# Moving the normalisation, the accumulation and layer-two buffers in a two-layer attention encoder

## The chip, the core and the metric

The kernel runs on one core of one Trainium2 chip. The metric is the device time in microseconds of one launch, from host input to output in the chip's memory, as a median over runs. The engines are TensorE (PE; its weight loads are shown apart as PEld), VectorE (DVE), ScalarE (ACT), GpSimd (POOL) and SyncE (SP), which issues the DMAs.

## What is computed

The reference is an encoder of two layers over 1024 tokens of width 1024, in fp32, with 256 memory tokens. Each layer normalises its input, projects it once, runs groups of attention heads, multiplies their joined output by SiLU of a gate, projects it and adds it to the input; a last RMSNorm follows.

```python
h = rmsnorm(x, norm_g)
... = _split(h @ w_in, SPLITS)
y = concatenate([heads of the layer, y_x], -1) * silu(gate)
return x + y @ w_out
```

In layer one the groups are A (six heads, window of 128 to each side, a bias by relative position, a learned sink in the softmax), B (six dense heads with normalised and rotated queries and keys) and X (four heads of cross-attention into the memory). In layer two they are C and X. C is differential attention, six heads with values of width 128:

```python
p = softmax(s + bias)
w = p[0] - lam * p[1]
y_c = rmsnorm(w @ v, subln_g) * (1.0 - lam_init)
```

## The kernel before

**Arithmetic.** TensorE is fed with fp32 numbers split into a high and a low part (the names end in h and l); a product is three matmuls (high·high, high·low, low·high), some with two where one side's low part is left out. A projection is 48 matmuls of 128x512: two halves of 512 tokens, each 24 matmuls into one accumulator `acc` (L292). Its weights come by DMA (`wr`), DVE makes the high part `wh` (L236), POOL or DVE the low part `wl` (L238).

**Projections as filling.** The projections of a layer are a list of jobs, with steps before which a job may not start (`after`). `jobs.pull(n)` runs the next n pieces of eight matmuls, `jobs.ensure(tag)` runs the list until a job is done. So attention steps and projections are mixed by hand in one program order; a scheduler then settles the order on each engine from readiness and priority, so the built order is not quite the source's.

**Attention steps.** `run_steps` (L432) takes a list of steps, each one block of 128 queries of a head (256 for A). In pass i it does, in this order:

- the hop of step i-1 (`word_copy`, L497): a DMA on SP that copies the finished map `e` to `er`, in the number format in which TensorE transposes it;
- s1 of step i: the scores on PE into an S bank (`sx`, `sb`, `sa`, `sc`), the row minimum on DVE, the exponential on ACT with the row sums, and the normalisation of the map: on DVE for X, on POOL for B and A (L1019, L1098). For C, DVE adds the bias while it takes the minimum (L1384), and after two exponentials (L1387) comes rz (L1391), a factor mr (L1393) and the combination of the two maps, e = e2 * mr + e1 (L1395);
- s3 of an older step: the product with the values on PE into an A bank (`ox`, `ob`, `oa`, `oc`) and its evacuation. Behind C's s3 lie two posts, each called in a pass of its own: sums of squares `ssqc` in a T bank (L1424), z from them on DVE (L1427), a power on POOL (L226); then the broadcast `rbcc` in a T bank (L1436) and O = O * rbcc on DVE (L1438);
- the first half of the step's filling (`fill` is 3 pieces for X, C and B's first head, 1 for the rest);
- the posts;
- s2 of an older step (lag 2, for most A and B steps 3): eight transposes of `er` in two groups into T banks (`te`, L514; `ta` for A), each copied out by ACT (PTh, L306) and DVE (PTl, L307);
- the second half of the filling.

**Buffers.** PSUM has three pairs: S (two of 128x1024), T and A (two of 128x512 each). T also takes the transposed values `tv` (L396) and the posts' tiles; A also takes the projections' `acc`. In SBUF, `er` has three buffers in both layers, and the rings of a layer are set in `open_main` (L349 to 354), for layer two Q with 6 (the queries `cq`), `sg` with 3 (a projection's split result), K 4, KL 2, V 2, gy 2 (the gates).

**Layer two's list of jobs** (from L1306) is xq0, xq1 (the queries of X), m0 to m3 (keys and values of the memory), the gates g6 and g7 for X, then per head k, q, v and gate, each not before a given step (q0 not before step 8, v0 not before step 9). `jobs.ensure("m1")` (L1344) runs the list up to m1 before the first of the eight X steps; the 48 C steps follow.

Of the kernel before, what the change touches and what calls it, by code (L numbers as in the profile page):

```python
# [38 lines left out]
SLOW = (4,)  # L39
XB = 0  # L40
ABLAG = 3
ER = 3
PRE = (range(2, 8), range(2, 4))
SPARE = 24

# [107 lines left out]
def encoder_kernel(ctx, tc, A):  # L153
    nc = tc.nc
# [33 lines left out]
    gq, nlam, gs, ls, le = (misc[:, a:b] for a, b in ((0, 1), (1, 2), (2, 3), (3, 5), (5, 7)))  # L188
# [32 lines left out]
    def stat(name, n=1, bufs=3):  # L221
        return sm.tile([P, n], F32, tag=name, name=name, bufs=bufs)
# [209 lines left out]
    def run_steps(steps, jobs, hooks=None):  # L432
        n = len(steps)
        posts = deque()
        p2 = p3 = 0
        for i in range(n + LAG + 1):
            if jobs is not None:
                jobs.step = i
            if hooks:
                hooks(i)  # L440
            if 0 < i <= n and steps[i - 1].hop:
                steps[i - 1].hop()
            if i < n:
# [12 lines left out]
            if jobs is not None:  # L456
                jobs.pull(f - f // 2)
            for q in list(posts):
                q.pop(0)()
                if not q:  # L460
                    posts.remove(q)
            if p2 < n and p2 + steps[p2].lag <= i:
                steps[p2].s2()
                p2 += 1
            if jobs is not None:
# [30 lines left out]

    def word_copy(M, e):  # L497
        def f():
            t = M.at.tile([P, 1024], F32R, tag="er", name="er", bufs=ER)
            dma(t.bitcast(F32), e[0])  # L500
            e[0] = t
        return f
# [39 lines left out]
    def x_steps(M, X, gates, fill, qtile, ydst):  # L542
        steps = []
        for qb in range(8):
# [5 lines left out]
            e = [None]  # L550
            st.fill = fill

            def s1(qb=qb, e=e):
                kh, kl = X["kh"], X["kl"]
                Sp = ps_s("sx").rearrange("p (h m) -> p h m", h=4)
                for h in range(4):
                    qt, qc = qtile(h, qb)
                    qk(Sp[:, XPOS[h], :], qt, qc, kh[:, h, :], kl[:, h, :], 0, MEM)
                mn = stat("mn4", 4)
                nc.vector.tensor_reduce(out=mn, in_=Sp, op=ALU.min, axis=AX.X)  # L560
                et = new_e(M)
                ev = et.rearrange("p (h m) -> p h m", h=4)
                z = stat("z4", 4)
                for h in range(4):
                    nc.scalar.activation(ev[:, h, :], Sp[:, h, :], AF.Exp, bias=mn[:, h:h + 1],
                                         scale=-1.0, accum_out=z[:, h:h + 1])
                rz = stat("rz4", 4)
                nc.vector.reciprocal(rz, z)
                for h in range(4):
                    nc.vector.tensor_scalar(out=ev[:, h, :], in0=ev[:, h, :], scalar1=rz[:, h:h + 1],  # L570
                                            scalar2=None, op0=ALU.mult)
                e[0] = et
            st.s1 = s1
            st.hop = word_copy(M, e)
            st.s2 = dense_s2(M, e, st)
# [94 lines left out]
    M = open_main(right, "right", 0)  # L670
# [133 lines left out]
    def load_q(store, src, h):  # L804
        store[h] = new_q(M, "q")
        dma(store[h], src[h])
# [68 lines left out]
    def gt(l, m, after=-1):  # L875
        add(l, jl, "g%d" % m, gate_job(m), after)
# [27 lines left out]
    jobs = Jobs(jl, ld)  # L904
# [73 lines left out]
    last_x = steps[7].s1  # L978

    def x7():  # L980
        last_x()
        jobs.ensure("bq0")
        load_q(Bq, bq_d, 0)
    steps[7].s1 = x7
    bgrp = {}
    if True:
        def b_step(h, qb):
# [8 lines left out]
            def s1(h=h, qb=qb, e=e):  # L996
                if qb == 2 and h < 5:
                    jobs.ensure("bq%d" % ((h + 1) // 2))
                    load_q(Bq, bq_d, h + 1)
                if h == NB0 and qb == 0:  # L1000
                    jobs.ensure("bq2")
                    open_ab()
                    jobs.ensure("aq0")
                    load_q(Aq, aq_d, 0)
                    a_bias(0)
                Sp = ps_s("sb")
                for j in range(2):
# [8 lines left out]
                nc.scalar.activation(et, Sp, AF.Exp, bias=mr, scale=nrq[:, qb, h:h + 1], accum_out=z)  # L1016
                rz = stat("rz")
                nc.vector.reciprocal(rz, z)  # L1018
                nc.gpsimd.tensor_tensor(out=et, in0=et, in1=rz.to_broadcast([P, 1024]), op=ALU.mult)  # L1019
                e[0] = et  # L1020
            st.s1 = s1
            st.hop = word_copy(M, e)
            st.s2 = dense_s2(M, e, st)
# [35 lines left out]
    if True:  # L1059
        def a_step(h, p):  # L1060
# [5 lines left out]
            def s1(h=h, p=p, e=e):  # L1066
# [23 lines left out]
                nc.vector.tensor_tensor(out=z, in0=z, in1=es, op=ALU.add)  # L1090
                rz = stat("rz2", 2)
                nc.vector.reciprocal(rz, z)
                for j in range(2):
                    qb = 2 * p + j
                    lo, hi = max(0, qb - 1) * P, min(8, qb + 2) * P
                    c = lo - (qb - 1) * P
                    ej = et[:, j, c:c + hi - lo]
                    nc.gpsimd.tensor_tensor(out=ej, in0=ej, in1=rz[:, j:j + 1].to_broadcast([P, hi - lo]), op=ALU.mult)  # L1098
                e[0] = et
            st.s1 = s1  # L1100

            def hop(p=p, e=e):
                t = M.at.tile([P, 1024], F32R, tag="er", name="er", bufs=ER)[:, :768]
# [203 lines left out]
        add(1, jl, "xq%d" % p, lambda w, p=p: proj_job(w, hT, S, half_q(Xq1, p, lambda m: m)))  # L1307
    for tag, src, run in mem_jobs(M, 1, memT, X):
        job(jl, tag, src, run)
    gt(1, 6)  # L1310
    gt(1, 7)
    for h in range(6):
        a = -1 if h == 0 else 8 + 8 * (h - 1)
        add(1, jl, "k%d" % h, ck_job(h), a)
        add(1, jl, "q%d" % h, lambda w, h=h: proj_job(w, hT, S, half_q(C[h], 0, lambda m: m)),
            8 if h == 0 else a + 4)
        if h < 5:
            add(1, jl, "v%d" % h, v_job(C[h], True), 9 if h == 0 else 8 + 8 * (h - 1) + 1)
            gt(1, h, 9 if h == 0 else a + 2)
# [29 lines left out]
    for h in range(6):  # L1349
        for qb in range(8):  # L1350
# [8 lines left out]
            def s1(h=h, qb=qb, e=e, grp=grp):  # L1359
# [20 lines left out]
                for m in range(2):  # L1380
# [6 lines left out]
                    nc.scalar.activation(et, et, AF.Exp, bias=mn[:, m:m + 1], scale=-1.0,  # L1387
                                         accum_out=z[:, m:m + 1])
                    es.append(et)
                rz = stat("rz")  # L1390
                nc.vector.reciprocal(rz, z[:, 1:2])  # L1391
                c = stat("mr")
                nc.vector.scalar_tensor_tensor(out=c, in0=z[:, 0:1], scalar=nlam, in1=rz,  # L1393
                                               op0=ALU.mult, op1=ALU.mult)
                nc.vector.scalar_tensor_tensor(out=es[0], in0=es[1], scalar=c, in1=es[0],  # L1395
                                               op0=ALU.mult, op1=ALU.add)
# [132 lines left out]
```

## Time and profile before

| | |
|---|---|
| median of three runs | 1284.13 us (1282.78 to 1285.4) |
| profiled execution | 1293.23 us |
| its span (first to last instruction) | 1291.4 us |
| its mean granted TensorE clock | 0.983 |
| moved by DMA | 198.85 MB, 154 GB/s on average |

Times of a view are microseconds from the start of the span. A row of instructions shows start, duration, engine, line, operation and tiles, and in brackets the wait ahead of it with the instruction that ended it. A row of waits shows who waited for whom, then the total, the number and the longest. By the starts of their matmuls on PE, layer one's scores and products lie between 66.7 us (the first `sx`) and 551.8 (the last `oa`), the first parts of its output projection (`pre`, L631) from 441.1, layer two's products `ox` end at 725.3, and its C steps lie between 707.4 (the first `sc`) and 1217.4 (the last `oc`).

### The profile page before, as it was taken

The page shows a single profiled execution, that of the slowest core. Times are in us where ns is not written, and L with a number is a line of the kernel's source. Part 1 is how long each engine was busy: PE and PEld are TensorE (multiplying, and loading weights), DVE is VectorE, ACT ScalarE, POOL GpSimd, SP SyncE. Part 2 cuts the span into 40 slices and gives each one's busy share as a digit, 9 for nine tenths or more (in the row PEclk, how much of TensorE's full clock was granted, in tenths as well). Part 3 has the DMA queues.
Part 4 walks back from the last instruction along what each step waited for, and adds up shares of the span by engine and source line. Part 5 has one row for each costly group of instructions (what it writes and reads, how often), then busy time and mean ns, then how long its engine had stood idle before and what let it go on. Part 6 is the DMA issues. An engine that isn't in the chain of part 4 may idle for free.

```text
span 1291.4 us, 19572 instructions
## 1 busy us (share of the span) xinstructions
PE 1231.4 (95%) x6806; PEld 1006.6 (78%) x6806; DVE 854.2 (66%) x1623; ACT 605.0 (47%) x1275; POOL 425.3 (33%) x390
## 2 busy tenths in 40 slices
PE   5989999999999899999999999999999999999998
PEld 4878888888887678877787787777777777876886
DVE  5566676477777787747466856776767676676444
ACT  6245464356566755633134534444444444464222
POOL 5024355356666654503032122231222122131100
PEclk9999999999999899999999999999999999997999
DMA  6654335545365555377544333342332323453263
GB/s 245 196 177 152 130 140 183 166 149 194 135 226 204 202 204 192 143 220 258 145 163 129 130 101 104 114 119 100 115 120 99 119 100 106 139 196 124 83 212 120
DMA packets 95646, 198.85 MB, mean 154 GB/s; under 512 B 11286, under 2 KB 30998, under 8 KB 95548
## 3 DMA queue, kind: packets, MB, share of 16 engines
q1 hardware_dynamic: 95548, 197.60, 45.9%
q8 instruction: 54, 0.88, 0.3%
q14 instruction: 44, 0.36, 0.1%
HBM read 78.80 MB, written 30.95 MB: 85 GB/s over the span
## 4 chain that ended last, share of the span: by engine, by line
PE 45%; DVE 4%; issue 2%; DMA 1%; ACT 1%; POOL 0%; POOLq 0%; SPq 0%; DVEq 0%; ACTq 0%
PE acc L292 22%; PE po L631 5%; PE oc L1409 5%; PE sc L1372 3%; PE te L514 3%; PE sc L1378 2%; PE pre L631 2%; DVE wh L236 1%; PE ssqc L1424 1%; PE ox L588 1%; DVE e L1395 1%; DVE O L1438 1%; ACT e L1387 1%; DMA wor<-in_w_out 0%; PE tv L396 0%
## 5 line engine op out<-in xcount | busy, mean ns | idle before, releaser
L292 PE MATMUL acc<-h,wh 128*128 128x512 f32 x1536 | 497.2, 399 | 5.9 <-DVE wh L236 2.0
L292 PEld LDWEIGHTS acc<-h,wh 128*128 128x128 f32 x1536 | 284.6, 190 | 64.7 <-issue 7.2
L292 PE MATMUL acc<-h,wl 128*128 128x512 f32 x768 | 307.1, 400 | 1.6 <-POOL wl L238 1.6
L238 POOL TENSOR_TENSOR wl<-wr,wh 128x512 fp32r<-128x512 f32 x96 | 125.9, 1313 | 283.6 <-DVE wh L236 144.5
L292 PEld LDWEIGHTS acc<-h,wl 128*128 128x128 f32 x768 | 145.7, 190 | 35.0 <-issue 5.8
L1387 ACT ACTIVATE e<-e,mn 128x1024 f32<-128x1024 f32 x96 | 110.2, 1149 | 130.4 <-DVE mn L1384 130.4
L307 DVE TENSOR_TENSOR PTl<-te,PTh 128x512 fp32r<-128x512 f32 x224 | 145.6, 684 | 32.4 <-ACT PTh L306 31.0
L306 ACT CAST PTh<-te 128x512 fp32r<-128x512 f32 x224 | 124.4, 588 | 76.4 <-PE te L514 71.9
L1384 DVE CUSTOM_DVE_ANT_0 e<-sc,toep 128x1024 f32<-128x1024 f32 x96 | 113.9, 1219 | 24.7 <-PE sc L1378 24.6
L1019 POOL TENSOR_TENSOR e<-e,rz 128x1024 f32<-128x1024 f32 x48 | 92.2, 1922 | 72.6 <-DVE rz L1018 68.8
L514 PEld LDWEIGHTS te<-identr,er 128*128 128x128 f32 x896 | 93.5, 144 | 26.9 <-DVE O L1438 12.2
L514 PE MATMUL te<-identr,er 128*128 128x128 f32 x896 | 102.8, 251 | 7.4 <-DVE O L1438 3.2
L236 DVE CAST wh<-wr 128x512 fp32r<-128x512 f32 x112 | 61.8, 554 | 38.6 <-PE acc L292 18.6
L226 POOL TENSOR_TENSOR rz<-z,nhalf 128x2 f32<-128x2 f32 x24 | 16.7, 697 | 198.5 <-DVE z L1427 192.6
L1016 ACT ACTIVATE e<-sb,mr,nrq 128x1024 f32<-128x1024 f32 x48 | 58.0, 1208 | 43.1 <-DVE mr L1015 34.1
L1409 PE MATMUL oc<-PTh,v 128*128 128x256 f32 x384 | 74.8, 288 | 0.0
L631 PE MATMUL po<-woh,yh 128*128 128x512 f32 (+1 forms) x176 | 67.9, 387 | 0.1
L631 PE MATMUL po<-woh,yl 128*128 128x512 f32 (+1 forms) x176 | 67.3, 383 | 0.0
L631 PE MATMUL po<-wol,yh 128*128 128x512 f32 (+1 forms) x176 | 67.3, 382 | 0.0
L1409 PEld LDWEIGHTS oc<-PTh,v 128*128 128x128 f32 x384 | 61.4, 191 | 6.2 <-issue 5.5
L1395 DVE SCALAR_TENSOR_TENSOR e<-e,mr 128x1024 f32<-128x1024 f32 x48 | 65.3, 1360 | 0.9
L1011 DVE TENSOR_REDUCE mn<-sb 128x1 f32<-128x1024 f32 x48 | 58.4, 1216 | 6.3 <-PE sb L483 6.1
(199 smaller groups left out, 2289.7 us busy)
## 6 DMA issues: line engine op xcount, KB each, us to landing
er<-e SPq DMA_DIRECT2D x112, 512.0 KB, 3.0
wr<-in_w_in SPq DMA_DIRECT2D x96, 256.0 KB, 2.8
ysc<-gy SPq DMA_DIRECT2D x16, 512.0 KB, 2.8
wor<-in_w_out SPq DMA_DIRECT2D x32, 256.0 KB, 3.7
cq<-sg SPq DMA_DIRECT2D x64, 128.0 KB, 2.4
ck<-sg SPq DMA_DIRECT2D x48, 128.0 KB, 2.4
er<-e SPq DMA_DIRECT2D x12, 384.0 KB, 2.6
xt<-in_x SPq DMA_DIRECT2D x8, 512.0 KB, 6.2
```

The source lines that it names most:

```text
L236: nc.vector.tensor_copy(hi, raw)
L238: (nc.vector if fast else nc.gpsimd).tensor_tensor(out=lo, in0=raw, in1=hi, op=ALU.subtract)
L292: lastmm[0] = nc.tensor.matmul(acc, a, b[:, k, c0:c0 + n], start=(i == 0), stop=(i == 23))
L306: nc.scalar.copy(hi, src)
L307: return nc.vector.tensor_tensor(out=lo, in0=src, in1=hi, op=ALU.subtract)
L514: nc.tensor.transpose(to[:, i * P:(i + 1) * P], e[0][:, k * P:(k + 1) * P], idt)
L631: lastmm[0] = nc.tensor.matmul(acc, a, b, start=(start and n == 0), stop=(stop and n == 2))
L1019: nc.gpsimd.tensor_tensor(out=et, in0=et, in1=rz.to_broadcast([P, 1024]), op=ALU.mult)
L1384: nc.vector.tensor_tensor_reduce(out=et, in0=Sp, in1=toeps[h][:, w0:w0 + 1024], scale=1.0, scalar=BIG, op0=ALU.add, op1=ALU.min, accum_out ...
L1387: nc.scalar.activation(et, et, AF.Exp, bias=mn[:, m:m + 1], scale=-1.0, accum_out=z[:, m:m + 1])
L1395: nc.vector.scalar_tensor_tensor(out=es[0], in0=es[1], scalar=c, in1=es[0], op0=ALU.mult, op1=ALU.add)
L1409: nc.tensor.matmul(acc, V[:, kt, v, :], pt[:, kt, :], start=(n == 0), stop=(n == 23))
```

## The change

Three things are edited.

First, in `run_steps` the normalisation is taken out of s1: each s1 returns it as `finish`, which is called after s2. Second, s3 goes behind the first half of the filling and the posts. Third, in layer two `er` gets two buffers instead of three, Q eight instead of six and `sg` five instead of three; gate 6 is listed right behind m1 (ahead of m2 and m3) and must be done before the steps start, and q0 may start at step 4 instead of 8.

```diff
@@ open_main
-        M.cfg = (dict(Q=(1024, 4), K=4, KL=4, V=1, gy=4, sg=3) if l == 0
-                 else dict(Q=(512, 6), K=4, KL=2, V=2, gy=2, sg=3))
+        M.cfg = (dict(Q=(1024, 4), K=4, KL=4, V=1, gy=4, sg=3, er=3) if l == 0
+                 else dict(Q=(512, 8), K=4, KL=2, V=2, gy=2, sg=5, er=2))
@@ run_steps
-                steps[i].s1()
+                finish = steps[i].s1()
+            f = steps[min(i, n - 1)].fill
+            if jobs is not None:
+                jobs.pull(f - f // 2)
+            for q in list(posts):
+                q.pop(0)()
+                if not q:
+                    posts.remove(q)
             if p3 < n and p3 + steps[p3].lag + 1 <= i:
                 st, p3 = steps[p3], p3 + 1
                 if st.s3 is not None:
...
                     r = st.s3()
                     if r:
                         posts.append(r)
-            f = steps[min(i, n - 1)].fill
-            if jobs is not None:
-                jobs.pull(f - f // 2)
-            for q in list(posts):
-                q.pop(0)()
-                if not q:
-                    posts.remove(q)
             if p2 < n and p2 + steps[p2].lag <= i:
                 steps[p2].s2()
                 p2 += 1
+            if finish:
+                finish()
+                finish = None
             if jobs is not None:
                 jobs.pull(f // 2)
@@ the s1 of C (those of X, B and A likewise)
-                rz = stat("rz")
-                nc.vector.reciprocal(rz, z[:, 1:2])
...
-                e[0] = es[0]
+                def finish():
+                    rz = stat("rz")
+                    nc.vector.reciprocal(rz, z[:, 1:2])
...
+                    e[0] = es[0]
+                return finish
@@ the jobs of layer two
     for tag, src, run in mem_jobs(M, 1, memT, X):
         job(jl, tag, src, run)
-    gt(1, 6)
+        if tag == "m1":
+            gt(1, 6)
     gt(1, 7)
...
-            8 if h == 0 else a + 4)
+            4 if h == 0 else a + 4)
...
-    jobs.ensure("m1")
+    jobs.ensure("m1", "g6")
```

In the changed kernel a line has another number, up to some 15 away, than before. The built orders show what moves. First, DVE in layer two, in a C step without s3; before (rz, mr and e as above; sg is the low part of a projection's result, O the scaled product of the pair before, PTl the low part of a transposed map):

```order
L1391 RECIPROCAL rz_10254<-mn_10121 128x1
L1438 SCALAR_TENSOR_TENSOR O_10169<-O_10169,misc_84,rbcc_10285 128x256
L1393 SCALAR_TENSOR_TENSOR mr_10256<-mn_10121,misc_84,rz_10254 128x1
L310 SCALAR_TENSOR_TENSOR sg_10276<-acc_10226,sg_10275 128x512
L1395 SCALAR_TENSOR_TENSOR e_10248<-e_10251,mr_10256,e_10248 128x1024
L307 TENSOR_TENSOR PTl_10210<-te_10290,PTh_10208 128x4x128
```

Now, from rz on in the same step:

```order
L1403 RECIPROCAL rz_10276<-mn_10095 128x1
L1440 SCALAR_TENSOR_TENSOR z2_10258<-ssqc_10255,es_10176 128x2
L1405 SCALAR_TENSOR_TENSOR mr_10278<-mn_10095,misc_84,rz_10276 128x1
L1407 SCALAR_TENSOR_TENSOR e_10232<-e_10235,mr_10278,e_10232 128x1024
L306 TENSOR_TENSOR PTl_10180<-te_10262,PTh_10178 128x4x128
```

The combination e stays ahead of PTl. The copy sg and the scaling O, which stood between rz and e, have left, and z2 of the earlier pair has come in.

Second, PE in layer one, at the first A step; before (te transposes of a B step, sa and sb scores of A and B):

```order
L514 MATMUL te_2640<-identr_74,er_2357 128x128 x4
L514 MATMUL te_2647<-identr_74,er_2357 128x128 x4
L483 MATMUL sa_2656<-ak0_2207,q_2546 128x256
L483 MATMUL sa_2656<-akl0_2209,q_2546 128x256
L483 MATMUL sb_2727<-bk0_1031,q_1865 128x512
L483 MATMUL sa_2656<-ak0_2207,q_2546 128x384
L483 MATMUL sa_2656<-akl0_2209,q_2546 128x384
```

Now:

```order
L517 MATMUL te_2644<-identr_74,er_2357 128x128 x4
L486 MATMUL sa_2656<-ak0_2235,q_2546 128x256
L486 MATMUL sa_2656<-akl0_2237,q_2546 128x256
L291 MATMUL acc_2670<-h_122,wh_2448 128x512
L291 MATMUL acc_2670<-h_123,wh_2448 128x512
L291 MATMUL acc_2670<-h_122,wl_2449 128x512
L291 MATMUL acc_2670<-h_122,wh_2448 128x512
L291 MATMUL acc_2670<-h_123,wh_2448 128x512
L486 MATMUL sa_2656<-ak0_2235,q_2546 128x384
```

Between the two score groups of the A step stand five matmuls of a projection where the score of the next B step stood, and the second group of transposes has moved away.

Third, PE in the same C step as in the first pair; before:

```order
L1436 MATMUL rbcc_10285<-ident_69,rz2_10206 128x128 x2
L514 MATMUL te_10290<-identr_74,er_10119 128x128 x4
L292 MATMUL acc_10317<-h_6363,wh_10100 128x512
L292 MATMUL acc_10317<-h_6364,wh_10100 128x512
L514 MATMUL te_10297<-identr_74,er_10119 128x128 x4
```

Now:

```order
L291 MATMUL acc_10238<-h_6365,wh_9917 128x512
L1437 MATMUL ssqc_10255<-ones2_76,sqc_10174 128x2 x2
L517 MATMUL te_10262<-identr_74,er_10093 128x128 x4
L517 MATMUL te_10269<-identr_74,er_10093 128x128 x4
L291 MATMUL acc_10238<-h_6366,wh_9917 128x512
```

The two groups of transposes stand together with the sums of squares ahead of them, where the broadcast rbcc stood ahead and projections lay between them.

More of the change, by code (lines that the diff above doesn't have):

```diff
@@ L41 @@
 ABLAG = 3
-ER = 3
 PRE = (range(2, 8), range(2, 4))
@@ L464, in run_steps @@
                 p2 += 1
+            if finish:
+                finish()
+                finish = None
             if jobs is not None:
@@ L498, in f @@
         def f():
-            t = M.at.tile([P, 1024], F32R, tag="er", name="er", bufs=ER)
+            t = M.at.tile([P, 1024], F32R, tag="er", name="er", bufs=M.cfg["er"])
             dma(t.bitcast(F32), e[0])
@@ L566, in s1 @@
                                          scale=-1.0, accum_out=z[:, h:h + 1])
[L567 to L572, printed above, removed]
+                def finish():
+                    rz = stat("rz4", 4)
+                    nc.vector.reciprocal(rz, z)
+                    for h in range(4):
+                        nc.vector.tensor_scalar(out=ev[:, h, :], in0=ev[:, h, :], scalar1=rz[:, h:h + 1],
+                                                scalar2=None, op0=ALU.mult)
+                    e[0] = et
+                return finish
             st.s1 = s1
@@ L980, in x7 @@
     def x7():
-        last_x()
+        r = last_x()
         jobs.ensure("bq0")
         load_q(Bq, bq_d, 0)
+        return r
     steps[7].s1 = x7
@@ L1016, in s1, with finish @@
                 nc.scalar.activation(et, Sp, AF.Exp, bias=mr, scale=nrq[:, qb, h:h + 1], accum_out=z)
-                rz = stat("rz")
-                nc.vector.reciprocal(rz, z)
-                nc.gpsimd.tensor_tensor(out=et, in0=et, in1=rz.to_broadcast([P, 1024]), op=ALU.mult)
-                e[0] = et
+                def finish():
+                    rz = stat("rz")
+                    nc.vector.reciprocal(rz, z)
+                    nc.gpsimd.tensor_tensor(out=et, in0=et, in1=rz.to_broadcast([P, 1024]), op=ALU.mult)
+                    e[0] = et
+                return finish
             st.s1 = s1
@@ L1089, in s1, with finish @@
                 nc.scalar.activation(es, mn, AF.Exp, bias=sinkb[:, h:h + 1], scale=1.0)
[L1090 to L1099, printed above, removed]
+                def finish():
+                    nc.vector.tensor_tensor(out=z, in0=z, in1=es, op=ALU.add)
+                    rz = stat("rz2", 2)
+                    nc.vector.reciprocal(rz, z)
+                    for j in range(2):
+                        qb = 2 * p + j
+                        lo, hi = max(0, qb - 1) * P, min(8, qb + 2) * P
+                        c = lo - (qb - 1) * P
+                        ej = et[:, j, c:c + hi - lo]
+                        nc.gpsimd.tensor_tensor(out=ej, in0=ej, in1=rz[:, j:j + 1].to_broadcast([P, hi - lo]), op=ALU.mult)
+                    e[0] = et
+                return finish
             st.s1 = s1
             def hop(p=p, e=e):
-                t = M.at.tile([P, 1024], F32R, tag="er", name="er", bufs=ER)[:, :768]
+                t = M.at.tile([P, 1024], F32R, tag="er", name="er", bufs=M.cfg["er"])[:, :768]
                 a, b = (P if p == 0 else 0), (768 - P if p == 3 else 768)
@@ L1389, in s1, with finish @@
                     es.append(et)
[L1390 to L1396, printed above, removed]
-                e[0] = es[0]
+                def finish():
+                    rz = stat("rz")
+                    nc.vector.reciprocal(rz, z[:, 1:2])
+                    c = stat("mr")
+                    nc.vector.scalar_tensor_tensor(out=c, in0=z[:, 0:1], scalar=nlam, in1=rz,
+                                                   op0=ALU.mult, op1=ALU.mult)
+                    nc.vector.scalar_tensor_tensor(out=es[0], in0=es[1], scalar=c, in1=es[0],
+                                                   op0=ALU.mult, op1=ALU.add)
+                    e[0] = es[0]
+                return finish
             st.s1 = s1
```

## Prediction

> **What bounds the kernel now.** I read the page first, for the engines' shares.
>
> ```profile
> span 1291.4 us, 19572 instructions
> PE 1231.4 (95%) x6806; PEld 1006.6 (78%) x6806; DVE 854.2 (66%) x1623; ACT 605.0 (47%) x1275; POOL 425.3 (33%) x390
> ```
>
> TensorE is the bound; 60 us of the span (1291.4 - 1231.4) are left to it as idle time. An edit that moves no matmul out can only win from those 60 us, from gaps hidden under the modelled ends of matmuls, and from stretches at a lower clock. So the second view was a table by stage (stretch, its length, PE busy, granted clock, DMA share, GB/s):
>
> ```profile
> 205.00:420.00 215.00, 209.26 (x1227) 1.00 0.53 180
> 420.00:444.00 24.00, 19.66 (x109) 0.82 0.55 193
> 444.00:562.00 118.00, 115.35 (x684) 0.99 0.53 185
> 632.00:650.00 18.00, 14.71 (x92) 0.91 0.44 127
> 650.00:718.00 68.00, 65.43 (x358) 1.00 0.47 149
> 842.40:924.80 82.40, 80.44 (x449) 1.00 0.34 111
> 1155.00:1165.70 10.70, 6.86 (x47) 1.00 0.72 243
> 646.90:650.30 3.40, 3.40 (x13) 0.51 0.61 163
> 1165.70:1182.70 17.00, 17.00 (x47) 0.50 0.33 113
> ```
>
> The first three rows are layer one's mixed A and B steps, with 5.74, 4.34 and 2.65 us of PE idle. Rows four and five are the start of layer two, with 3.29 and 2.57 us. The sixth is one head of layer two: 1.96 us idle in 82.4. Row seven is the end of layer two's attention, 3.84 us idle. The last two rows lie in stretches where the granted clock was half. Third, who PE waited for in three of these stretches (205 to 420, 632 to 718, 718 to 1150; total us, times, longest):
>
> ```profile
> PE sb L483 <- ACT e L1016: 1.7, 2, 0.9
> PE acc L292 <- DVE gy L417: 1.3, 2, 0.8
> PE sa L483 <- ACT e L1016: 1.0, 1, 1.0
> PE oa L1135 <- ACT PTa L306: 0.6, 2, 0.3
> ```
>
> ```profile
> PE acc L292 <- DVE yt L596: 1.5, 2, 1.1
> PE sx L483 <- ACT e L565: 1.4, 1, 1.4
> PE ox L588 <- DVE ckl L1280: 1.0, 1, 1.0
> ```
>
> ```profile
> PE tv L396 <- DVE PTl L307: 4.2, 4, 1.1
> PE te L514 <- DVE O L1438: 3.2, 8, 0.6
> ```
>
> Nothing large is left: these are waits of about a microsecond each, nearly all for a PSUM bank that ACT or DVE has not emptied.
>
> **The change, part by part.** No arithmetic is removed or added. Three things move.
>
> *The normalisation (finish).* The words of the change put it behind the step's copies out of PSUM. In layer two the built order on DVE, shown above, does not do that: the combination (e) still stands ahead of the copy PTl; what left the stretch is the copy of the projection (sg), and the statistic of the earlier pair (z2 in place of O) came in. I cost the moved combination at nothing in both layers. The hop that follows it takes this long:
>
> ```profile
> er<-e SPq DMA_DIRECT2D x112, 512.0 KB, 3.0
> ```
>
> In layer two the copy is read two steps later, some 20 us (an 82.4 us head has eight steps), so 3.0 us and a wait for one of now two er buffers stay covered; were that cover gone, each step would pay up to 3.0 us. What queues behind a waiting hop on SP are weight loads and row copies for projections a step or more away.
>
> *The accumulation (s3) behind the first half of the fill.* In the order shown for TensorE at the first A step, projections now stand where the next score sb stood, and the trace shows what sb cost there:
>
> ```profile
> 253.79 1.20 ACT L1016 ACTIVATE e<-sb,mr,nrq 128x1024 f32<-128x1024 f32 x1
> 253.92 0.28 PE L483 MATMUL sa<-akl,q 128*128 128x256 f32 x1
> 255.13 0.50 PE L483 MATMUL sb<-bk,q 128*128 128x512 f32 x1 [0.93 <-ACT e L1016]
> ```
>
> A score needs one of two S banks, which the exponential was still reading. The two groups of waits on ACT e (1.7 + 1.0 us) should go, and part of the waits for gy and for PTa, since projections now lie between ta and oa: of 5.74 + 2.65 us I take 4.0 (ends 0 and 8.4). The stretch 420 to 444 has no projections left to fill with in either order, so its 4.34 us stay.
>
> In layer two the pieces around te move, as the third pair of orders shows. The second te needs the T bank that rbcc held till O, and now one that ssqc holds till z2. One such step of before:
>
> ```profile
> 904.79 0.73 PE L292 MATMUL acc<-h,wh 128*128 128x512 f32 x2
> 908.36 0.18 ACT L1387 ACTIVATION_READ_ACCUMULATOR e<-e,mn 128x1 f32 x1
> 908.58 0.16 DVE L1391 RECIPROCAL rz<-mn 128x1 f32<-128x1 f32 x1 [0.47 <-ACT e L1387]
> 908.69 0.55 PE L514 MATMUL te<-identr,er 128*128 128x128 f32 x4
> 909.46 0.47 DVE L1438 SCALAR_TENSOR_TENSOR O<-O,misc,rbcc 128x256 f32<-128x256 f32 x1
> 909.99 0.53 PE L514 MATMUL te<-identr,er 128*128 128x128 f32 x4 [0.22 <-DVE O L1438]
> ```
>
> O ended at 909.93. z2 would follow rz directly and, at an estimated 0.16 like rz (both a few elements wide), end near 908.9; PE comes to its second te after 908.69 plus the first four transposes, about 909, so the wait goes. Of 3.2 us I take 2.0, since some of the eight were set by weight copies that stand ahead of rz. The larger wait, 4.2 us of tv, stays: it ends with PTl, and PTl still waits for the combination.
>
> ```profile
> 891.01 1.72 DVE L1395 SCALAR_TENSOR_TENSOR e<-e,mr 128x1024 f32<-128x1024 f32 x1
> 892.65 1.28 DVE L307 TENSOR_TENSOR PTl<-te,PTh 128x512 fp32r<-128x512 f32 x2
> 893.38 0.33 PE L396 MATMUL tv<-ident,vraw 128*128 128x128 f32 x1 [1.05 <-DVE PTl L307]
> ```
>
> Ends for this term: a gain of 7.4 (both rows) and the loss of the third rival. At the end of layer two (1155 to 1165.7) DVE's order is the same as before, two weight subtractions ahead of the maps' first pass, so I take 0 of the 3.84 us.
>
> *The start of layer two.* Gate 6 (48 matmuls, as any projection) now precedes the cross-attention steps, so they start with their keys landed and with fill ready; eight Q and five sg buffers let both xq projections finish, where six and three made the last halves wait for steps that had not begun. Projections are only exchanged in time: q0, released at step 4 and not 8, fills the hole that gate 6 leaves. I take all 3.29 us of 632 to 650, the 1.0 us of ox, and 1.7 us for the half-clock stretch that follows them (half of 3.4): 6.0 (ends 3.3 and 7.6). Against it, two pairs of cross-attention steps now have both ox groups around a te with no projection between; each can make the next projection wait for its A bank as in the row acc <- yt, about 1.0 each: -2.0 (ends 0 and -4).
>
> Sum: 4.0 + 2.0 + 6.0 - 2.0 = 10.0 us. The profiled execution took 1293.23 us, 1.8 more than its span and 9.1 above the median of 1284.13; no row says what the 9.1 are, so I take the 10.0 off the median: **1274.1**, written as 1274.
>
> **The clock.** Half clock from 1165.7 to 1182.7 cost 8.5 us, right behind idle times of 3.84 us in 10.7, of which the longest single wait was about 2 us:
>
> ```profile
> PE sc L1372 <- DVE mn L1384: 2.0, 1, 2.0
> ```
>
> [...]
>
> **Rivals.**
>
> 1. *The clock gives more* (0.17). If the waits ahead of 1165.7 shrink a little, the 17 us stretch at half clock goes too: 8.5 + 3.84 more, 1261.8. For: the dips stand behind the densest waits. Against: DVE's order there is unchanged.
>
> 2. *The waits are only rearranged* (0.17). S, T and A keep two banks each, so waits taken off one place come back at the next. Then the terms 4.0 and 2.0 are nothing and -2.0 doubles: 6.0 - 4.0 = 2.0, 1282.1, no change. [...] This is also the case in which the change does not do what its words say.
>
> 3. *Slower* (0.13): z2 now stands behind rz, and rz behind the second exponential, in each of the 24 pairs of layer two, with no projections between the two te. If ACT has one more copy ahead (0.59, like PTh) and DVE one weight copy (0.43), the second te waits about 1.02 - 0.2 = 0.8 us each time: 24 x 0.8 = 19 us against gains of 4.0 + 6.0 - 2.0 = 8, so 1295. It decides from 0.33 us a step (8/24).
>
> ```profile
> 909.27 0.59 ACT L306 CAST PTh<-te 128x512 fp32r<-128x512 f32 x1 [0.73 <-PE te L514]
> 907.68 0.43 DVE L236 CAST wh<-wr 128x512 fp32r<-128x512 f32 x1
> ```
>
> **The numbers.** The forecast itself (1266 to 1281) has 0.53. Faster by over 0.2% (2.6 us, about what a measurement of this kernel can tell from no change) holds it and rival 1: 0.70; within: 0.17; slower: 0.13. The range 1260 to 1286 takes in rivals 1 and 2 and leaves out rival 3 and some of the deeper ends of rival 1, under 2 in 10.
>
> **What would show it.** Right: no wait of sb on ACT e between A and B steps; 632 to 650 with under 1 us idle and full clock; te <- O gone; tv <- PTl still near 1 us a head. Wrong: tv <- PTl gone, a row te <- z of many microseconds, waits of acc on yt above 3 us, or a span that moved only where the clock did.

## The result and the profile after

The changed kernel takes 1276.73 us (median of 9 runs, 1271.98 to 1279.18), before 1285.23 (9 runs beside them); the ratio is 0.9928, with a 95% interval of 0.9909 to 0.9946. That is 8.5 us faster, where 10 were forecast. The page of the changed kernel:

```profile
span 1275.8 us, 19602 instructions
PE 1218.1 (95%) x6806; PEld 1008.8 (79%) x6806; DVE 850.7 (67%) x1623; ACT 602.9 (47%) x1275; POOL 426.6 (33%) x390
```

The span is 15.6 us shorter (1291.4 - 1275.8), nearly twice the difference of the medians. And PE's *busy* time fell by 13.3 us with the same 6806 matmuls. Both need an explanation.

To see where the time went, both kernels are cut at the same matmuls: the first `sx`, the last `oa`, the first `sc`, the first `sc` of the last head, the last `oc`. The table by stage of before (stretch, length, busy of PE, PEld, DVE, ACT and POOL, granted clock, DMA share, GB/s; the last row is one head):

```profile
66.70:551.80 485.10, 466.21 (x2699) 390.39 (x2697) 341.54 (x707) 271.88 (x611) 249.26 (x213) 0.98 0.50 174
551.80:707.40 155.60, 147.91 (x782) 123.44 (x781) 94.25 (x168) 54.72 (x144) 31.53 (x32) 0.99 0.59 184
707.40:1118.10 410.70, 401.61 (x2221) 318.76 (x2220) 285.45 (x504) 182.40 (x335) 97.06 (x89) 1.00 0.34 112
1118.10:1217.40 99.30, 95.46 (x513) 75.32 (x512) 66.61 (x117) 48.93 (x92) 20.17 (x18) 0.91 0.40 137
871.50:953.90 82.40, 80.43 (x449) 64.03 (x448) 57.44 (x101) 36.19 (x66) 19.71 (x19) 1.00 0.34 111
```

The same of the changed kernel:

```profile
66.80:551.20 484.40, 461.27 (x2703) 392.07 (x2701) 344.24 (x707) 271.97 (x611) 247.49 (x213) 0.98 0.50 174
551.20:704.50 153.30, 146.13 (x779) 122.08 (x777) 91.51 (x165) 53.81 (x143) 31.68 (x33) 0.99 0.61 183
704.50:1103.10 398.60, 395.28 (x2220) 319.46 (x2219) 284.20 (x509) 181.91 (x337) 98.94 (x88) 1.00 0.36 118
1103.10:1202.10 99.00, 94.24 (x515) 75.39 (x514) 64.62 (x115) 48.09 (x92) 21.13 (x20) 0.93 0.39 134
862.90:942.90 80.00, 79.16 (x449) 64.30 (x448) 56.60 (x101) 36.01 (x66) 20.62 (x18) 1.00 0.35 115
```

Layer one is 0.7 us shorter, the start of layer two 2.3, the first five heads of layer two 12.1 (some 2.4 a head), the last head 0.3. So nearly all of it came in the heads, where 2.0 had been forecast.

**What is in a head.** The last row of each table has 449 matmuls. PE's idle time fell from 1.97 us to 0.84, its busy time by 1.27. A matmul's row is longer than its share of PE, as two neighbours in the changed kernel's timeline show:

```profile
444.59 0.39 PE L636 MATMUL pre<-woh,yh 128*128 128x512 f32 x1
444.81 0.39 PE L636 MATMUL pre<-wol,yh 128*128 128x512 f32 x1
```

The first lasts 0.39 us and the next starts after 0.22. So a short wait of the next one is hidden under the row ahead and counted as busy; only the length of the stretch shows all of it. In the five heads of before, 18 groups of te stand behind a projection and start on average 0.56 us after its last matmul, where one matmul of a projection starts 0.23 us after another: that is some 6.0 us of waiting, against 3.2 in the row of waits. The waits of PE in the changed kernel from 718 to 1103 us are one row:

```profile
PE tv L395 <- DVE PTl L306: 3.3, 4, 0.8
```

The row te <- O (3.2, 8 times) is gone. A step with the broadcast, on PE and DVE (one row is DVE's):

```profile
907.51 0.38 PE L1449 MATMUL rbcc<-ident,rz 128*128 128x128 f32 x2
907.65 0.36 PE L1422 MATMUL oc<-PTh,v 128*128 128x256 f32 x1
...
910.48 0.28 PE L1422 MATMUL oc<-PTh,v 128*128 128x256 f32 x1
910.60 0.79 PE L517 MATMUL te<-identr,er 128*128 128x128 f32 x8
908.00 0.48 DVE L1451 SCALAR_TENSOR_TENSOR O<-O,misc,rbcc 128x256 f32<-128x256 f32 x1
```

Between rbcc and te lies the accumulation oc, 2.95 us (910.60 - 907.65). O has read its bank by 908.48, so all eight transposes run through.

**Layer one** has its own new waits (66.8 to 551.2 us):

```profile
PE pre L636 <- DVE yt L428: 3.7, 1, 3.7
...
PE acc L291 <- DVE yt L601: 2.0, 1, 2.0
```

The accumulation now stands right ahead of the next user of the pair A, which waits until DVE has emptied the bank. In the longer one DVE was busy with the input of `pre`, and yt stood behind it:

```profile
448.29 3.62 DVE L309 SCALAR_TENSOR_TENSOR yl<-yr,yh 128x512 fp32r<-128x512 f32 x2 [0.36 <-ACT yh L308]
451.94 0.43 DVE L428 TENSOR_TENSOR yt<-oa,yt 64x256 f32<-64x256 f32 x1
```

With each of the two comes a stretch at half clock, the first from 1.5 us behind the end of its wait, the second from the last microsecond of its wait:

```profile
185.20:188.60 3.40, 3.40 (x11) 2.73 (x11) 3.31 (x8) 1.82 (x3) 3.03 (x4) 0.50 0.96 390
...
451.40:458.20 6.80, 5.78 (x20) 4.70 (x21) 4.61 (x9) 1.67 (x4) 1.09 (x2) 0.50 0.44 143
```

Before has none at these two places. It has others in layer one, and over all of layer one the granted clock is 0.98 in both tables.

**The clock in all runs.** Nearly every run has its span and mean granted clock. As an estimate, span times (1 - clock) is what the lower clock cost it, and span times clock what the span would be at full clock (the clock has three digits, so each is rounded to within 0.6 us). Medians over the runs of before that have a clock (70) and those of the changed kernel (15, with a later set below):

| | time | span at full clock | cost of the clock |
|---|---|---|---|
| before | 1284.94 | 1271.9 | 11.5 |
| changed | 1276.73 | 1256.2 | 17.9 |

By this estimate the change removes 15.7 us at full clock, and the clock takes back 6.4 (5.0 to 8.9 at 95%, resampled). The estimate charges too much for the clock, since it takes every microsecond at half clock as half lost. Over the 70 runs of before the span grows by 0.70 us for each microsecond of this cost, over the 15 of the changed kernel by 0.71; at that rate the change removes some 12.7 us and the clock takes back 4.5. The excess lies in layer one. Seven profiled executions have layer one in the same order (before, e3, e4, e5, e8, e9 and e11 below): it takes 481.9 us with 3.4 us at half clock in e11 and 485.1 with 20.4 in before, so 17 us more at half clock cost 3.2 and not 8.5. At the end of layer two the estimate holds: the last head of before took 99.3 us with 17.1 at half clock, that of e3 92.1 with 3.4. Differences at full clock and by the clock below are by this estimate, so their size is an upper value.

The clock also explains most of the 9.1 us by which the profiled execution of before stood above its median: at a clock of 0.983 it is charged with 22.0 us of its 1291.4, some 10 more than the median run, or 7 at the rate of 0.70.

### The profile page after: what moved, and what is told of

The parts are those of the page before. It is cut to its first block, busy times and chain, and to the rows that moved or that the text cites. A ratio compares the mean times of both kernels' runs of the same rounds, so it can differ in the third digit from the quotient of the medians.

```text
span 1275.8 us, 19602 instructions
## 1 busy us (share of the span) xinstructions
PE 1218.1 (95%) x6806; PEld 1008.8 (79%) x6806; DVE 850.7 (67%) x1623; ACT 602.9 (47%) x1275; POOL 426.6 (33%) x390
## 4 chain that ended last, share of the span: by engine, by line
PE 46%; DVE 3%; issue 1%; ACT 1%; DMA 1%; POOL 0%; POOLq 0%; SPq 0%; DVEq 0%; ACTq 0%
PE acc L291 24%; PE po L636 5%; PE oc L1422 5%; PE sc L1383 3%; PE te L517 2%; PE sc L1389 2%; PE pre L636 2%; PE ox L593 1%; PE ssqc L1437 1%; DMA wor<-in_w_out 1%; PE tv L395 1%; PE sx L486 1%; DVE e L1407 1%; DVE mr L1405 0%; ACT e L568 0%
## 5 line engine op out<-in xcount | busy, mean ns | idle before, releaser
L291 PEld LDWEIGHTS acc<-h,wh 128*128 128x128 f32 x1536 | 285.2, 189 | 73.7 <-issue 11.6
L517 PEld LDWEIGHTS te<-identr,er 128*128 128x128 f32 x896 | 90.9, 143 | 14.7 <-issue 3.5
L517 PE MATMUL te<-identr,er 128*128 128x128 f32 x896 | 97.9, 247 | 4.0 <-issue 1.7
L235 DVE CAST wh<-wr 128x512 fp32r<-128x512 f32 x112 | 55.5, 498 | 30.9 <-PE acc L291 8.9
L1454 POOL TENSOR_TENSOR gy<-O,gy 128x256 f32<-128x256 f32 x24 | 31.1, 1297 | 108.9 <-DVE O L1451 83.1
L1407 DVE SCALAR_TENSOR_TENSOR e<-e,mr 128x1024 f32<-128x1024 f32 x48 | 62.5, 1303 | 1.1
```

The costliest lines, as they stand in the source:

```text
L291: lastmm[0] = nc.tensor.matmul(acc, a, b[:, k, c0:c0 + n], start=(i == 0), stop=(i == 23))
L517: nc.tensor.transpose(to[:, i * P:(i + 1) * P], e[0][:, k * P:(k + 1) * P], idt)
```

## The experiments

The theory tested, T: the accumulation stands between the broadcast and the transposes, so te finds its T bank free. The prediction had the same bank and the same wait, but gave as the reason only that ssqc now stands where rbcc stood. Rivals: N, the normalisation's place does it; B, layer two's buffers and gate do it. Of each kernel: median, ratio to before with its interval, span at full clock, cost of the clock. Each ratio is to the runs of before beside the kernel, with a median of 1285.17 us for e1 to e4, 1284.56 for e5 to e8 and 1284.86 for the others.

| kernel | us | ratio | full clock | clock |
|---|---|---|---|---|
| e1, accumulation alone | 1280.70 | 0.9964 (0.9944 to 0.9983) | 1263.5 | 16.0 |
| e2, normalisation alone | 1283.57 | 0.9986 (0.9963 to 1.0008) | 1270.6 | 11.5 |
| e3, layer-two buffers and gate alone | 1284.37 | 0.9985 (0.9965 to 1.0006) | 1269.2 | 12.2 |
| e4, posts ahead of the accumulation | 1288.86 | 1.0027 (1.0008 to 1.0045) | 1275.4 | 11.6 |
| e5, layer one in its old order | 1273.95 | 0.9913 (0.9886 to 0.9939) | 1259.1 | 13.3 |
| e6, combination behind PTl | 1276.59 | 0.9930 (0.9903 to 0.9956) | 1255.2 | 19.1 |
| e7, normalisation back | 1278.59 | 0.9944 (0.9922 to 0.9966) | 1261.9 | 15.3 |
| e8, accumulation alone, layer two only | 1279.92 | 0.9949 (0.9931 to 0.9968) | 1263.9 | 14.0 |
| a1, changed kernel again | 1276.63 | 0.9905 (0.9872 to 0.9937) | 1255.8 | 19.1 |
| e9, e5 and e6 | 1272.79 | 0.9892 (0.9864 to 0.9920) | 1256.1 | 15.3 |
| e10, e9 with layer one's normalisation deferred | 1273.17 | 0.9887 (0.9856 to 0.9918) | 1256.4 | 15.9 |
| e11, rbcc in a bank of A | 1285.71 | 1.0002 (0.9980 to 1.0024) | 1270.5 | 13.5 |

### Each part alone: e1, e2, e3

e1 moves the accumulation only: against the changed kernel, `finish` runs right behind s1, and layer two's settings are those of before.

```diff
                 finish = steps[i].s1()
+            if finish:
+                finish()
+                finish = None
             f = steps[min(i, n - 1)].fill
```

> Only the accumulation is moved behind the first half of the filling and the posts; the normalisation stays in s1 and layer two keeps its old buffers and job order. Theory T (the accumulation of 24 matmuls now stands between the broadcast rbcc and the transposes te, so te finds its T bank free): about -8 us against before, heads of layer two at 80 us where before has 82.4. Rival N (the normalisation's place does it): within 2 us of before. Rival B (layer two's buffers and gate do it): within 2 us of before.

e2 defers the normalisation only: against the changed kernel, s3 stands ahead of the filling again, with layer two's settings of before.

```diff
+            if p3 < n and p3 + steps[p3].lag + 1 <= i:
+                st, p3 = steps[p3], p3 + 1
...
             f = steps[min(i, n - 1)].fill
```

> Only the normalisation is deferred behind the copies out of PSUM; the accumulation stays where it was, layer two keeps its buffers and job order. Theory T: within 2 us of before, heads of layer two at 82.4 us. Rival N: -6 us or more, heads at 80 us. Rival B: within 2 us of before.

e3 is the kernel before with only layer two's edits:

```diff
-                 else dict(Q=(512, 6), K=4, KL=2, V=2, gy=2, sg=3))
+                 else dict(Q=(512, 8), K=4, KL=2, V=2, gy=2, sg=5, er=2))
...
-    jobs.ensure("m1")
+    jobs.ensure("m1", "g6")
```

> Only layer two's rings (er 2, Q 8, sg 5), gate 6 ahead of m2 and the start of q0. Theory T: -1 to -3 us, all of it between the first cross-attention score and the first C score of layer two, heads at 82.4 us. Rival N: within 1 us of before. Rival B: -6 us or more.

One head of layer two by the table by stage, in e1:

```profile
866.20:946.50 80.30, 79.04 (x449) 64.23 (x448) 56.62 (x101) 36.01 (x66) 20.61 (x18) 1.00 0.35 114
```

The same head in e2:

```profile
866.30:948.70 82.40, 80.42 (x449) 63.96 (x448) 56.65 (x102) 36.21 (x66) 18.78 (x19) 1.00 0.34 111
```

And in e3:

```profile
870.20:952.70 82.50, 80.55 (x450) 63.99 (x450) 57.52 (x101) 36.14 (x66) 19.82 (x19) 1.00 0.34 112
```

The five heads together take 410.7 us in before, 402.8 in e1, 410.8 in e2 and 411.0 in e3. Alone, only the accumulation shortens them: T for the place, against N and B. The time of e1 fell by only 4.5 us where 8 were expected: at full clock it is 8.4 us below before, and the clock takes about half of that back (16.0 against 11.5). e3 is 2.7 below at full clock and 0.8 in time, which its interval does not tell from nothing; the same holds for e2's 1.6.

### What makes te wait: e4 and e11

If te waits for the bank of rbcc, taking rbcc away from te should do as well as moving the accumulation. e4 calls the posts ahead of the accumulation and the filling, in the kernel before:

```diff
+            for q in list(posts):
+                q.pop(0)()
+                if not q:
+                    posts.remove(q)
             if p3 < n and p3 + steps[p3].lag + 1 <= i:
...
                 jobs.pull(f - f // 2)
-            for q in list(posts):
-                q.pop(0)()
-                if not q:
-                    posts.remove(q)
             if p2 < n and p2 + steps[p2].lag <= i:
```

> The kernel before with only the posts (the sums of squares and the broadcast of the pair before) called ahead of the accumulation and of the first half of the filling; accumulation, normalisation and buffers as before. Theory T: it also takes rbcc away from the place right ahead of te, so the heads of layer two come to about 80 us and the time to -8 us or more. Rivals N and B: within 2 us of before.

e11 gives rbcc another bank:

```diff
-                        T = ps_t("rbcc")
+                        T = ps_a("rbcc")
```

> The kernel before with one edit: the broadcast rbcc of C is put into a bank of the pair A instead of T. Theory T (te waited for the T bank that rbcc held until O): no wait of te for O is left, and the heads come to 80.5 to 81.5 us unless a projection waits for that A bank instead; -3 to -8 us. Rival P (te is late for another reason, such as the transposed map er or ACT's copies): heads stay at 82.4 us and the time within 2 us of before.

PE's waits in the heads of e4 (718 to 1118 us):

```profile
PE rbcc L1436 <- DVE PTl L307: 9.5, 9, 1.6
PE tv L396 <- DVE PTl L307: 5.6, 4, 1.4
```

And of e11 (718 to 1115 us):

```profile
PE tv L396 <- DVE PTl L307: 5.6, 4, 1.4
PE acc L292 <- DVE O L1438: 4.5, 10, 0.8
```

In both, no wait of te for O is left, so that was its cause. But T in the broad form that e4's expectation gave it is wrong: rbcc then comes soon behind the transposes of the step before and waits for the T bank that PTl has not yet emptied, 9.5 us in place of 3.2, and e4 is 3.7 us slower than before. In e11 a projection waits for O in the pair A, and the time is that of before. With two banks a pair, it is not enough to part rbcc from te, and not enough to have the accumulation behind rbcc, which e4 has too. In the changed kernel rbcc has the 16 matmuls of the filling ahead of it, so that PTl has emptied its bank, and the 2.95 us of the accumulation, which already has its bank, behind it. In e4 those 16 stand on the other side, between the accumulation and te.

### Layer one and the clock: e8, e5

e8 is e1 in layer two alone; e5 is the changed kernel with layer one's pass as before. Both branch in `run_steps`:

```diff
+            if l == 0:
...
+            else:
...
```

> The kernel before with only the accumulation moved, and only in layer two. Theories T and C: heads at 80.3 us, full-clock time about 10 us below before and no more half-clock time than before, so about -9 us against before, that is 4 us better than the same move in both layers. Rival L: less than -4.5 us, what the move in both layers gave.

> The changed kernel with layer one put back in its old order (accumulation ahead of the filling, normalisation in s1); layer two as changed. Theory C (the change gains nothing in layer one, and the waits that it makes there for the A banks, 2.2 us in the cross-attention steps and 3.9 us where the projections run out, each bring a stretch at half clock): 3 to 5 us below the changed kernel, about 1273, with no half-clock stretch near 185 and none near 451 us. Rival L (layer one's accumulation behind the filling gains the 4.0 us of the prediction): 2 to 4 us above the changed kernel.

e8 against e1: 1279.92 and 1280.70 us, 1263.9 and 1263.5 at full clock. So the accumulation's move alone gains nothing in layer one. But e8's expectation failed too: -4.6 against the before beside it (1284.56) and not -9, since it gained 8.0 and not 10 at full clock and its clock cost 14.0 against 11.5 in before (a difference that the spread of its runs does not tell from nothing). e5 came out near what theory C expected: 2.8 us below the changed kernel (4.8 below to 0.3 above, resampled), 2.9 worse at full clock, 4.6 better by the clock. Its trace has no half-clock stretch near 185 or 451 us, as C said, and layer one takes 482.9 us in it, against 484.4 in the changed kernel.

### The combination behind PTl: e6, and the normalisation back: e7

```diff
-                    nc.vector.scalar_tensor_tensor(out=es[0], in0=es[1], scalar=c, in1=es[0],
-                                                   op0=ALU.mult, op1=ALU.add)
+                    with (tc.issue_after(lastpt[0].ins) if lastpt[0] is not None else nullcontext()):
+                        nc.vector.scalar_tensor_tensor(out=es[0], in0=es[1], scalar=c, in1=es[0],
+                                                       op0=ALU.mult, op1=ALU.add)
```

> The changed kernel with the combination e of the two maps of C held behind the second copy PTl on DVE, as the words of the change have it. Theory T (the wait tv for PTl is made by the combination ahead of PTl): the wait of about 1.1 us a head goes, heads at 79 us instead of 80, -4 to -6 us against the changed kernel. Rival D (DVE's next pass over the scores then comes later and PE waits for an S bank instead): within 1 us of the changed kernel or slower, with waits of sc for mn or e in each step.

e6 holds the combination behind s2's last instruction on DVE, as the diff shows. One head of it:

```profile
862.10:941.60 79.50, 79.33 (x449) 64.38 (x448) 53.94 (x101) 35.91 (x66) 17.45 (x18) 1.00 0.36 116
```

And PE's waits for PTl from 718 to 1101 us:

```profile
PE tv L396 <- DVE PTl L307: 0.7, 4, 0.2
```

The combination made that wait, as said: 3.3 us became 0.7. This head gains 0.5, not 1, and the five heads together only 0.6 (398.6 in the changed kernel):

```profile
703.00:1101.00 398.00, 396.45 (x2221) 319.99 (x2220) 275.68 (x510) 181.64 (x337) 85.41 (x87) 1.00 0.36 117
```

So the row of waits, which overlooked two thirds of te's gain, promises four times too much here (2.6). The time of e6 is that of the changed kernel (1276.59): 1.0 less at full clock, 1.2 more by the clock. The expected 4 to 6 us failed.

e7 calls `finish` right behind s1 in the changed kernel, as e1 does.

> The changed kernel with the normalisation back in s1; the accumulation, layer two's rings and job order as changed. Theory T (the deferral is worth nothing): within 1.5 us of the changed kernel. Rival N2 (the deferral is worth something once the accumulation is moved, since the three parts alone summed to less than the whole): 2 to 4 us above the changed kernel.

At full clock e7 takes 1261.9 us (1259.6 to 1264.0 over its 8 runs), the changed kernel 1256.2 (1253.2 to 1257.9 over its 15): the ranges do not meet. So by the estimate the deferral is worth 5.7 us at full clock once the accumulation is moved, though 1.3 alone. In time it is 1.9, and the two intervals overlap. In the five heads, where the clock is full, it is 3.0 (401.6 to 398.6 us), and PE's waits of tv for PTl there fall from 5.1 to 3.3:

```profile
703.30:1104.90 401.60, 395.20 (x2221) 319.32 (x2220) 285.92 (x509) 182.01 (x337) 98.79 (x88) 1.00 0.36 117
```

So of the 12.1 us in the heads of the changed kernel, 9.1 are the accumulation's and 3.0 the deferral's beside it. Waits of PE in layer one of e7 that are shorter or gone in the changed kernel:

```profile
PE sa L486 <- DVE mn L1090: 2.8, 4, 1.4
...
PE ob L1039 <- DVE PTl L306: 2.0, 3, 1.5
```

In the changed kernel the same two groups are 0.8 and 0.3:

```profile
PE sa L486 <- DVE mn L1090: 0.8, 2, 0.4
...
PE ob L1039 <- DVE PTl L306: 0.3, 1, 0.3
```

But the longest wait of the changed kernel in layer one, 3.7 us of pre for yt, is short in e7, and there is no half-clock stretch near 451 us in its trace or in that of e1:

```profile
PE pre L636 <- DVE yt L428: 0.4, 1, 0.4
```

The wait of 2.0 for yt comes with the moved accumulation alone (2.1 in e1 and e7), that of 3.7 only with the deferral beside it.

### On one chip: a1, e9, e10

> The changed kernel again, on the chip of the next three, to compare them directly: 1275 to 1279 us. Theory C expects its mean granted clock at 0.985 to 0.987, lower than that of the kernel before on this chip, and again stretches at half clock right behind the two longest waits for A banks in layer one.

> Layer one in its old order, layer two as changed and with the combination behind PTl. Theories C and T add up: layer two some 1.5 us shorter than with the combination ahead of PTl, layer one with less half-clock time; 1271 to 1274 us, 3 to 5 us below the changed kernel on this chip. Rival (the clock takes back what the waits give, wherever they go): within 1.5 us of the changed kernel.

> As the kernel with layer one in its old order and the combination behind PTl, but with layer one's normalisation deferred, its accumulation where it was. Theory C (layer one's end is set by its waits around each bank, whatever the order): within 2 us of that kernel. Rival F (the deferral itself gains in layer one): 2 us or more below it.

e10 differs from e9 in one call, `finish` behind s2 in layer one. In a1 the stretches are there again, behind the same two waits (2.1 and 3.3 us):

```profile
185.60:192.50 6.90, 6.90 (x22) 5.78 (x21) 4.25 (x11) 1.82 (x3) 5.07 (x5) 0.51 0.73 275
455.30:458.70 3.40, 3.13 (x12) 2.44 (x12) 2.46 (x5) 0.58 (x1) 0.73 (x1) 0.50 0.35 96
```

The traces of e5 and e9 have neither stretch; that of e10 has one of 3.4 us at 191.2, so such a stretch can also come without the moved accumulation. e9 is 3.8 us below a1 by the medians, though the intervals of their ratios overlap. All runs together tell more: the kernels with both the accumulation and the normalisation moved in layer one (changed, a1, e6: 21 runs) have a median of 1276.73, those with the accumulation left there (e5, e9, e10: 18 runs) 1273.09; the difference of 3.6 has a 95% interval of 1.2 to 4.9, resampled. At full clock the former are 1.6 better (not clear of nothing); the clock costs them 3.9 more (1.9 to 7.0). The two sets also differ in how many have the combination behind PTl, whose worth in time e6 did not tell from nothing. e7, with the accumulation moved in layer one but the normalisation in s1, pays 15.3 for the clock, no more than e5, e9 and e10 together (15.2). So the 3.9 are shown for the two moves in layer one together, not for the accumulation by itself. e10 is not told from e9. Both lie below before, and by the medians below the changed kernel; e9 has a ratio of 0.9892 to before.

## Why the prediction came out near, and where it was off

The total (10.0 us forecast, 8.5 measured) is a sum of terms that were off in both directions. That it came so near is luck: the heads brought some 10 us more than forecast, and layer one, the start of layer two and the clock together as much less.

- **te and O in layer two: 2.0 forecast, about 9 measured in the trace** (of 12.1 in the heads; the rest is the normalisation's, below). The place was right (e1, e8), and so was the cause of the wait, a T bank held until O (e4, e11). Why it goes was half of it: the prediction looked at the step where ssqc took the place of rbcc, and not at the step where rbcc now stands, where the accumulation covers it. The step that failed was the price: "Of 3.2 us I take 2.0". The row of waits holds only what reaches beyond the modelled end of the matmul ahead (3.2 of some 6.0 us in before); the end of 7.4 took in no more than that row and tv's. From the lengths of a head, 82.4 and 80.4 in e7, it is 2.0 a head.
- **A and B steps: 4.0 forecast, 0.7 measured in all of layer one.** The waits of sb for ACT e left, as forecast (none is left of sb; one of sa, 1.7, is), but pre <- yt (3.7), acc <- yt (2.0) and others came, and two of them come with half-clock stretches. This is the second rival, waits only rearranged, in layer one. The rival itself fell for layer two.
- **Start of layer two: 6.0 - 2.0 = 4.0 forecast, 2.3 measured** in the trace, and 0.8 (not clear of nothing) in time by e3. The 6.0 was too high: waits of acc for weights (1.1 and 0.8) and of ox for ckl (1.2) remain. The 2.0 taken off did not come, for no wait of acc for yt is left there. The sign that was named for this term, under 1 us idle and full clock from 632 to 650, did not come either; idle are 1.89 us, and a half-clock stretch of 3.4 us is still there (the traces of e6 and e7 have none, so it is not certain in either order):

```profile
632.00:650.00 18.00, 16.11 (x76) 13.08 (x75) 6.14 (x13) 1.57 (x3) 1.27 (x1) 0.91 0.38 113
```

- **End of layer two: 0 forecast, 0.3 measured.** But its clock is part of the clock's cost below.
- **The normalisation at nothing.** Right alone (e2), wrong beside the moved accumulation: 3.0 us in the heads, 5.7 in all by the estimate at full clock, though in time not told from nothing (e7). That PTl would still wait for the combination was right: tv <- PTl stayed, at 0.8 a time for 1.1, and e6 removed it by order.
- **The clock: a gain of 1.7 forecast, a loss of 6.4 by the estimate, some 4.5 at the rate of 0.70.** The prediction let the clock follow the waits at the start of layer two alone, and did not price the waits that the change makes elsewhere.
- **Taking the 10.0 off the median** and not off the profiled execution was right: the 9.1 us were mostly the clock.

The third rival, te waiting for z2 behind rz, cannot be seen as a row. Eight te right behind ssqc last 0.93 in one step of the changed kernel, against the 0.79 above:

```profile
899.40 0.93 PE L517 MATMUL te<-identr,er 128*128 128x128 f32 x8
899.58 0.16 DVE L1440 SCALAR_TENSOR_TENSOR z<-ssqc,es 128x2 f32<-128x2 f32 x1 [0.35 <-PE ssqc L1437]
```

That is about 0.14 us a step, under the 0.33 from which it would have decided. Why the changed kernel's clock costs 6.4 us is shown in part: some 3.9 go with the accumulation and the normalisation moved together in layer one. The rest, 15.2 in e5, e9 and e10 against 11.5 in before, has no shown cause; their traces have longer half-clock stretches at the end of layer two, here that of e9:

```profile
1147.20:1157.50 10.30, 9.68 (x26) 5.79 (x26) 8.17 (x15) 4.60 (x8) 2.53 (x3) 0.50 0.27 95
```

And that of e3:

```profile
1160.10:1163.50 3.40, 3.40 (x19) 3.40 (x18) 3.40 (x3) 1.35 (x3) 3.40 (x3) 0.50 0.72 246
```

All seven traces with the accumulation moved and layer two's buffers and gate (changed, a1, e5, e6, e7, e9, e10) have 10.2 to 13.7 us at half clock there; with the accumulation alone e1 has 3.4 and e8 6.8; e2, e3, e4 and e11 have 3.4 each. But the profiled execution of before had 17.1, and no run takes this end apart.

## What to carry to other kernels

Price a repeating wait by the length of its stretch, not by the row of waits: the row of te held 3.2 us and its removal brought 9, while 2.6 us off the row of tv brought 0.6. When two banks are shared by several kinds of work, look for the place where work that needs no new bank stands on both sides of a tile that is emptied late; here, moving that tile to a place with such work on one side only, or to another pair, only moved the wait. And look at the granted clock beside times: this change gained some 13 to 16 us at full clock and gave about a third of it back.

## What the runs showed of the hardware that was not expected

In the traces of before and the changed kernel, each of the ten half-clock stretches inside the kernel lasted 3.4 us or two to five times that (6.8, 10.2, 13.7 and 17.1 us). In the 7 us ahead of each, PE had waited: the longest time there from the start of one matmul to the start of the next was 1.3 to 4.1 us, where 0.23 is the median of all. Not every such wait brought one: that of tx for xs near 604 us, 2.0 from start to start in before and 2.1 in the changed kernel, did in neither. Nor does every such stretch cost the same: by the lengths above, a microsecond at half clock cost 0.2 us in layer one (3.2 us for 17, before against e11) and 0.5 at the end of layer two (7.2 for 13.7, before against e3).
